# Scaling rows on VectorE ahead of an identity transpose, in place of fp32 matmuls with a diagonal matrix

## The chip, the cores and the metric

One Trainium2 chip, one core. The time is device microseconds (us) of one execution. The engines are TensorE (PE, with its weight loads PEld), VectorE (DVE), ScalarE (ACT), GpSimd (POOL) and SyncE (SP), whose queue issues nearly all transfers. PE's clock has two levels, 1.2 and 2.4 GHz; the profile gives the granted clock as a share of the higher.

## What is computed

One layer of a conditioned decoder trunk on x (256 tokens x 2048 channels, fp32), everything in fp32:

```python
mod = cond @ w_ada[l] + b_ada[l]
sh1, sc1, gt1, sh2, sc2, gt2 = jnp.split(mod, N_MOD, axis=-1)
h = rms_norm(x, g_pre_mix[l]) * (1.0 + sc1) + sh1
y = token_mixing(h, ...)                       # w_in, three branches, gates, w_out
x = x + gt1 * rms_norm(y, g_post_mix[l])       # first residual
h = rms_norm(x, g_pre_ffn[l]) * (1.0 + sc2) + sh2
y = conv_ffn(h, ...)                           # w_up, causal convolution, gelu gate, w_down
x = x + gt2 * rms_norm(y, g_post_ffn[l])
```

rms_norm divides each token's row by the root of its mean square. The two places of the change are the two lines that make h.

## The kernel before

Tokens lie on the partitions for norms and residuals (two halves tt of 128 tokens), channels lie on the partitions for the products. So x (and the residual x2) has to be turned: quarter q of the channels (512) is a tile of 128 x 2 x 512, and its transpose a PSUM tile of four blocks of 128 channels x 256 tokens.

Norm and transpose are one step before. `rstd_from_sums` makes the factor r of each row (reduce and reciprocal on DVE, L195 and L197, root on ACT, L196). `diag_of` (L203) multiplies the identity by r on DVE into d, 128x128 for each half of the tokens. `scaled_transpose` (L210, matmul at L214) multiplies each 128x128 block of x by d, eight matmuls for a quarter; the product is the transposed block with its columns scaled. `make_h2` has the same loop again for quarter 0 (L795), into two PSUM tiles. An fp32 matmul shows as two records on PE, and the trace names these `ptx<-d,x`.

For the input, `x_stats` (L384) makes sums of squares, r1 and d1; `x_transpose(q)` (L391) makes the eight matmuls, ACT copies them out (xn, L394), and `make_h` applies scale and shift and splits into high and low part, hh and hl. For the residual, `residual(tt)` (L771) adds yg*r2 to x (L775, four of 128x512), takes sums of squares on ACT (L201), r3, and d2 for that half. `make_h2(q)` then makes for each of four blocks h2h on ACT (L799), h2f on DVE (L800) and h2l on DVE (L801).

The products are split in three: high x high, low x high, high x low (`mm_b` L231 to L233, `mm_a` L245 to L247). All weights come through SP's queue into four 1 MB buffers (raw), are split by ACT (wh, L274) and DVE (wl, L275; six buffers of each), and used by PE. The conditioning's GEMVs run on PE (gemv, L313) or DVE (L348, L350), and `fin_col` (fin, L286) turns their sums into s and sh columns.

The order of work is a list of items (weight loads with their uses) and calls between them, written out at the end of the kernel; `x_transpose(1..3)` go into a side queue that is served between items, `make_h2` is called twice at the first products of the up-projection and twice later. Parts of the code run at high priority (`out_evac` and `residual` in the last item of the output projection). From this a scheduler fixes each engine's stream when the kernel is built; every engine then runs its stream strictly in order. PSUM tiles of this kind (ps_acc) have three buffers.

Of the kernel before, what the change touches and what calls it, by code (L numbers as in the profile page):

```python
# [46 lines left out]
def kernel(  # L47
# [39 lines left out]

# [1 line left out]
    crow = cp.tile([16, P], F32, name="crow")  # L89
# [51 lines left out]

    # constants that depend on shapes alone
    rcnt = cp.tile([P, 4, 16], F32, name="rcnt")
# [47 lines left out]

# [1 line left out]
    def rstd_from_sums(r, ss, tt):  # L193
# [8 lines left out]

    def diag_of(d, r, tt):  # L203
        nc.vector.tensor_scalar(d[:, tt], ident, r[:, tt:tt + 1], None, op0=ALU.mult)

    def load_sqrt(after):
        """the table of the square root, once `after` is there."""
        nc.scalar.activation(warm, after, AF.Sqrt, bias=eps, scale=0.0)

    def scaled_transpose(xq, d, name):  # L210
        pt = acc_ps(name)
        for a in range(4):
            for tt in range(2):
                nc.tensor.matmul(pt[:, a, tt * 128:tt * 128 + 128],  # L214
                                 xq[:, tt, a * 128:(a + 1) * 128], d[:, tt], start=True, stop=True)
        return pt

# [4 lines left out]
    def mm_b(ps, w, act, first, last):  # L222
        """out channels on partitions: ps[:, nb, :] += w[:, nb*128:].T @ act."""
        n = len(w)
        for i, (wh, wl) in enumerate(w):
            xh, xl = act(i)
            for nb in range(4):
                s = slice(nb * 128, nb * 128 + 128)
                st = first and i == 0 and nb % 2 == 0
                sp = last and i == n - 1  # L230
                nc.tensor.matmul(ps[:, nb], wh[:, s], xh, start=st, stop=False, skip_group_check=True)  # L231
                nc.tensor.matmul(ps[:, nb], wh[:, s], xl, start=False, stop=False, skip_group_check=True)  # L232
                nc.tensor.matmul(ps[:, nb], wl[:, s], xh, start=False, stop=sp, skip_group_check=True)  # L233

    def mm_a(ps, w, act, first, last, tts=(0, 1)):
        """tokens on partitions: ps[:, tt, :] += act[:, tt].T @ w."""
        n = len(w)
        psv = ps.rearrange("p (a b) t -> p a (b t)", a=2)
        for i, (wh, wl) in enumerate(w):
            xh, xl = act(i)  # L240
            for tt in tts:
                s = slice(tt * 128, tt * 128 + 128)
                st = first and i == 0
                sp = last and i == n - 1
                nc.tensor.matmul(psv[:, tt], xh[:, s], wh, start=st, stop=False)  # L245
                nc.tensor.matmul(psv[:, tt], xh[:, s], wl, start=False, stop=False)  # L246
                nc.tensor.matmul(psv[:, tt], xl[:, s], wh, start=False, stop=sp)  # L247

# [1 line left out]
    items = []  # L250
# [30 lines left out]

# [1 line left out]
    def fin_col(src, scale, sec, kt0, n):  # L283
# [14 lines left out]
    def ada_pe(sec, kt0, n):  # L298
        """items: one section's columns kt0*128.., summed over rows on the tensor engine."""
        w = n * P  # L300
# [24 lines left out]
    def ada_dve(sec, kt0, n):  # L325
        """the same, summed over rows on the vector engine."""
        w = n * P
# [48 lines left out]

# [1 line left out]
    ss1 = cp.tile([P, 2, 4], F32, name="ss1")  # L378
    xn = {}

    r1 = cp.tile([P, 2], F32, name="r1")
    d1 = cp.tile([P, 2, P], F32, name="d1", tag="diag")

    def x_stats():  # L384
        for tt in range(2):
            for q in range(4):
                sum_squares(xq[q][:, tt], ss1, q, tt)
            rstd_from_sums(r1, ss1, tt)
            diag_of(d1, r1, tt)

    def x_transpose(q):  # L391
        pt = scaled_transpose(xq[q], d1, "ptx")
        xn[q] = p4(f"xn{q}")
        nc.scalar.activation(xn[q], pt, AF.Copy)  # L394
        del xq[q]
# [19 lines left out]

# [1 line left out]
    part = {}  # L417
# [36 lines left out]
    def block_use(name, kt0, nk, lo, hi):  # L454
        """rows kt0.. of a block's sum over the rows lo to hi."""
        def use(hl_):
# [34 lines left out]
    def block_items(names, lo, hi):  # L491
        """one item for as many neighbouring blocks as make a full load."""
        m = max(1, 4 // (hi - lo))
        while names:
            g = [names[0]]
            while len(g) < min(m, len(names)) and block_cols(names[len(g)]) == block_cols(g[0]) + 512 * len(g):
                g.append(names[len(g)])
            for kt0, nk in pieces(lo, hi):
                w_item(w_in, kt0, nk, block_cols(g[0]), *[block_use(x_, kt0, nk, lo, hi) for x_ in g])
            names = names[len(g):]  # L500
# [7 lines left out]

# [1 line left out]
    yh, yl = {}, {}  # L510
# [197 lines left out]

# [1 line left out]
    mh, ml = {}, {}  # L710
# [19 lines left out]

# [1 line left out]
    ss2 = cp.tile([P, 2, 4], F32, name="ss2")  # L732
# [38 lines left out]
    def residual(tt):  # L771
# [6 lines left out]
        rstd_from_sums(r3, ss3, tt)  # L778
        if tt == 0:
            late["d2"] = cp.tile([P, 2, P], F32, name="d2", tag="diag")  # L780
        diag_of(late["d2"], r3, tt)

    def make_h2(q):
        hh[q], hl[q] = p4(f"h2h{q}", dt=F32R), p4(f"h2l{q}", dt=F32R)
        hf = p4(f"h2f{q}")
        d = late["d2"]
        if q:
            pt = scaled_transpose(x2[q], d, "ptx2")
            pts = [pt[:, o] for o in range(4)]
        else:  # L790
            two = [acc_ps(f"ptx2_{i}") for i in range(2)]
            pts = [two[o // 2][:, (o % 2) * 2] for o in range(4)]
            for o in range(4):
                for tt in range(2):
                    nc.tensor.matmul(pts[o][:, tt * 128:tt * 128 + 128], x2[q][:, tt, o * 128:o * 128 + 128],  # L795
                                     d[:, tt], start=True, stop=True)
        for o in range(4):
# [4 lines left out]

# [1 line left out]
    zc = {}  # L804
# [30 lines left out]
    def up_item(j, half, kt0, lo, hi):  # L835
        """rows kt0.. of a block's sum over the rows lo to hi."""
        key = (j, half)
# [78 lines left out]

# [1 line left out]
    def call(fn):  # L918
        items.append(dict(kind="call", use=fn))

    def mix(a, b, lead=0, skip=0):
        """spread the items of b among those of a, from `skip` to `lead` items before the end."""
        res, bi, n = [], 0, max(1, len(a) - lead - skip)
# [217 lines left out]
```

## Time and profile before

| | us |
|---|---|
| median of three runs | 1440.17 (1439.54 to 1443.15) |
| span of the profiled execution | 1438.6 |
| PE busy | 1399.5 (97%) |
| DVE busy | 1075.6 (75%) |
| ACT busy | 689.0 (48%) |

The profiled execution is given by its span, the time from its first to its last record; the median of the runs is 1.6 us above it. Busy shares are means over stages with different limits, so the sections below go by stretch. In a timeline each row has start, duration, engine, line, operation, result and sources, shape and count, and in brackets how long the engine sat idle before and what ended that. Matmuls are pipelined, so the step from one row to the next is what a row costs, not its duration. ps_up is the up-projection, ps_g the gates' projection, ps_out the output projection.

### The profile page before, as it was taken

What the parts mean: (1) busy time and instruction counts of PE and PEld (TensorE: products, weight loads), DVE (VectorE), ACT (ScalarE), POOL (GpSimd) and SP (SyncE); (2) the same over time, 40 slices, a digit from 0 to 9 for tenths busy, and PEclk for the clock granted to TensorE, in tenths of its full rate; (3) what the DMA queues carried; (4) which work ended last, traced back from release to release, by engine and by line L of the source; (5) the groups of instructions that cost most, each with busy time, mean ns of one, the idle gap of its engine ahead of it and who ended that gap; (6) DMA issues with size and microseconds to landing.
All of it is one profiled execution on the core that took longest, in us unless ns stands there. A gap on an engine that the chain in (4) does not pass through costs nothing.

```text
span 1438.6 us, 24104 instructions
## 1 busy us (share of the span) xinstructions
PE 1399.5 (97%) x10079; PEld 1308.7 (91%) x10079; DVE 1075.6 (75%) x1349; ACT 689.0 (48%) x879; POOL 3.6 (0%) x12
## 2 busy tenths in 40 slices
PE   4999999999999999998999999999999999999997
PEld 3798999999999999887999989898989899999996
DVE  1289878789769977877878876868686766666677
ACT  4552534576744444345346654444444444445453
POOL 0000000000000000000000000000000000000000
PEclk9999999999999999999999999999999999999999
DMA  9799878855877788987976676676676665555551
GB/s 322 288 323 325 295 247 306 276 174 192 303 263 272 271 319 288 345 307 249 364 266 203 207 258 238 207 250 231 220 252 214 238 208 200 178 184 191 183 176 59
DMA packets 183036, 355.76 MB, mean 247 GB/s; under 512 B 5960, under 2 KB 20872, under 8 KB 182928
## 3 DMA queue, kind: packets, MB, share of 16 engines
q1 hardware_dynamic: 182076, 353.07, 72.0%
q8 instruction: 79, 1.29, 0.4%
q10 hardware_dynamic: 852, 1.16, 0.2%
q14 instruction: 29, 0.24, 0.0%
HBM read 352.11 MB, written 2.10 MB: 246 GB/s over the span
## 4 chain that ended last, share of the span: by engine, by line
PE 90%; DMA 4%; DVE 3%; ACT 1%; issue 1%; SPq 0%; DVEq 0%; ACTq 0%
PE ps_up L232 12%; PE ps_up L231 12%; PE ps_up L233 12%; PE ps_g L231 6%; PE ps_g L233 6%; PE ps_g L232 6%; PE ps_dn L246 6%; PE ps_dn L245 6%; PE ps_dn L247 6%; PE ps_out L245 2%; PE ps_out L246 2%; PE ps_out L247 2%; DMA raw<-in_w_in_dram 2%; PE ps_br L231 2%; PE ps_br L232 2%; PE ps_br L233 2%
## 5 line engine op out<-in xcount | busy, mean ns | idle before, releaser
L274 ACT ACTIVATE wh<-raw 128x1024 fp32r<-128x1024 f32 x476 | 489.9, 1037 | 637.7 <-PE ps_up L232 227.1
L275 DVE TENSOR_TENSOR wl<-raw,wh 128x1024 fp32r<-128x1024 f32 x476 | 565.0, 1197 | 243.9 <-ACT wh L274 243.1
L231 PE MATMUL ps_up<-h2h,wh 128*128 128x256 f32 x1408 | 400.2, 284 | 1.2 <-ACT h2h L799 0.8
L232 PE MATMUL ps_up<-h2l,wh 128*128 128x256 f32 x1408 | 399.4, 284 | 0.9 <-DVE h2l L801 0.9
L233 PE MATMUL ps_up<-h2h,wl 128*128 128x256 f32 x1408 | 399.1, 283 | 0.0
L231 PEld LDWEIGHTS ps_up<-h2h,wh 128*128 128x128 f32 x1408 | 270.9, 192 | 2.2 <-ACT h2h L799 0.9
L232 PEld LDWEIGHTS ps_up<-h2l,wh 128*128 128x128 f32 x1408 | 270.8, 192 | 2.1 <-DVE h2l L801 1.4
L233 PEld LDWEIGHTS ps_up<-h2h,wl 128*128 128x128 f32 x1408 | 270.8, 192 | 0.0
L231 PE MATMUL ps_g<-hh,wh 128*128 128x256 f32 x768 | 220.9, 288 | 2.8 <-ACT wh L274 2.8
L233 PE MATMUL ps_g<-hh,wl 128*128 128x256 f32 x768 | 219.0, 285 | 2.6 <-DVE wl L275 2.5
L232 PE MATMUL ps_g<-hl,wh 128*128 128x256 f32 x768 | 218.7, 285 | 0.0
L231 PEld LDWEIGHTS ps_g<-hh,wh 128*128 128x128 f32 x768 | 148.8, 194 | 4.8 <-ACT wh L274 3.8
L233 PEld LDWEIGHTS ps_g<-hh,wl 128*128 128x128 f32 x768 | 148.7, 194 | 3.6 <-DVE wl L275 3.6
L232 PEld LDWEIGHTS ps_g<-hl,wh 128*128 128x128 f32 x768 | 148.7, 194 | 0.3 <-issue 0.2
L245 PE MATMUL ps_dn<-wh,ah 128*128 128x512 f32 x352 | 137.8, 392 | 0.0
L246 PE MATMUL ps_dn<-wl,ah 128*128 128x512 f32 x352 | 137.0, 389 | 0.0
L247 PE MATMUL ps_dn<-wh,al 128*128 128x512 f32 x352 | 136.9, 389 | 0.0
L350 DVE SCALAR_TENSOR_TENSOR accb<-raw,cond,accb 128x512 f32<-128x512 f32 (+1 forms) x147 | 105.8, 720 | 10.4 <-DMA raw<-in_w_ada_dram 10.2
L350 DVE SCALAR_TENSOR_TENSOR acca<-raw,cond,acca 128x512 f32<-128x512 f32 (+1 forms) x155 | 111.9, 722 | 0.1
L245 PEld LDWEIGHTS ps_dn<-wh,ah 128*128 128x128 f32 x352 | 66.1, 188 | 14.0 <-issue 0.5
L246 PEld LDWEIGHTS ps_dn<-wl,ah 128*128 128x128 f32 x352 | 66.1, 188 | 13.9 <-issue 0.5
L247 PEld LDWEIGHTS ps_dn<-wh,al 128*128 128x128 f32 x352 | 66.1, 188 | 13.8
(237 smaller groups left out, 1700.3 us busy)
## 6 DMA issues: line engine op xcount, KB each, us to landing
raw<-in_w_up_dram SPq DMA_DIRECT2D x88, 1024.0 KB
raw<-in_w_ada_dram SPq DMA_DIRECT2D x84, 1024.0 KB
raw<-in_w_in_dram SPq DMA_DIRECT2D x54, 1024.0 KB
raw<-in_w_down_dram SPq DMA_DIRECT2D x44, 1024.0 KB
raw<-in_w_in_dram SPq DMA_DIRECT2D x24, 768.0 KB
raw<-in_w_out_dram SPq DMA_DIRECT2D x16, 1024.0 KB
raw<-in_w_ada_dram SPq DMA_DIRECT2D x16, 768.0 KB
x<-in_x_dram SPq DMA_DIRECT2D x8, 512.0 KB
```

Of the source, the lines that this page charges most:

```text
L231: nc.tensor.matmul(ps[:, nb], wh[:, s], xh, start=st, stop=False, skip_group_check=True)
L232: nc.tensor.matmul(ps[:, nb], wh[:, s], xl, start=False, stop=False, skip_group_check=True)
L233: nc.tensor.matmul(ps[:, nb], wl[:, s], xh, start=False, stop=sp, skip_group_check=True)
L245: nc.tensor.matmul(psv[:, tt], xh[:, s], wh, start=st, stop=False)
L246: nc.tensor.matmul(psv[:, tt], xh[:, s], wl, start=False, stop=False)
L247: nc.tensor.matmul(psv[:, tt], xl[:, s], wh, start=False, stop=sp)
L274: nc.scalar.activation(h[:, :n], it["raw"][:, k:k + n, cs], AF.Copy)
L275: nc.vector.tensor_tensor(l[:, :n], it["raw"][:, k:k + n, cs], h[:, :n].bitcast(F32), op=ALU.subtract)
L350: nc.vector.scalar_tensor_tensor(a, raw[:, kk], sc, a, op0=ALU.mult, op1=ALU.add)
```

## The change

`diag_of` and `scaled_transpose` go, and with them the tiles d1 and d2. `scale_rows` multiplies rows by r on DVE (128x512, one half of the tokens of one quarter), and `transpose_rows` is a PE transpose against the identity. For the input the rows are scaled in place in `x_stats`, all four quarters behind each r. For the residual x2 must stay, so `make_h2(q)` scales into a new tile xs of one quarter, both halves, and transposes that. 64 fp32 matmuls are replaced by 64 transposes. Comments were taken out as well, so line numbers of the changed kernel are 4 or 5 lower after line 208.

```diff
+    def scale_rows(dst, src, r, tt):
+        nc.vector.tensor_scalar(dst[:, tt], src[:, tt], r[:, tt:tt + 1], None, op0=ALU.mult)
-    def diag_of(d, r, tt):
-        nc.vector.tensor_scalar(d[:, tt], ident, r[:, tt:tt + 1], None, op0=ALU.mult)
...
-    def scaled_transpose(xq, d, name):
-        pt = acc_ps(name)
-        for a in range(4):
-            for tt in range(2):
-                nc.tensor.matmul(pt[:, a, tt * 128:tt * 128 + 128],
-                                 xq[:, tt, a * 128:(a + 1) * 128], d[:, tt], start=True, stop=True)
-        return pt
+    def transpose_rows(dst, src, tt, a):
+        nc.tensor.transpose(dst[:, tt * 128:tt * 128 + 128], src[:, tt, a * 128:(a + 1) * 128], ident)
...
     def x_stats():
         for tt in range(2):
             for q in range(4):
                 sum_squares(xq[q][:, tt], ss1, q, tt)
             rstd_from_sums(r1, ss1, tt)
-            diag_of(d1, r1, tt)
+            for q in range(4):
+                scale_rows(xq[q], xq[q], r1, tt)
...
     def x_transpose(q):
-        pt = scaled_transpose(xq[q], d1, "ptx")
+        pt = acc_ps("ptx")
+        for a in range(4):
+            for tt in range(2):
+                transpose_rows(pt[:, a], xq[q], tt, a)
...
         rstd_from_sums(r3, ss3, tt)
-        if tt == 0:
-            late["d2"] = cp.tile([P, 2, P], F32, name="d2", tag="diag")
-        diag_of(late["d2"], r3, tt)
...
         hf = p4(f"h2f{q}")
-        d = late["d2"]
+        xs = p4("xs", (2, 512))
         if q:
-            pt = scaled_transpose(x2[q], d, "ptx2")
+            pt = acc_ps("ptx2")
             pts = [pt[:, o] for o in range(4)]
         else:
             two = [acc_ps(f"ptx2_{i}") for i in range(2)]
             pts = [two[o // 2][:, (o % 2) * 2] for o in range(4)]
-            for o in range(4):
-                for tt in range(2):
-                    nc.tensor.matmul(pts[o][:, tt * 128:tt * 128 + 128], x2[q][:, tt, o * 128:o * 128 + 128],
-                                     d[:, tt], start=True, stop=True)
+        for tt in range(2):
+            scale_rows(xs, x2[q], r3, tt)
+        for o in range(4):
+            for tt in range(2):
+                transpose_rows(pts[o], xs, tt, o)
```

The scheduler's streams differ in a few places. The first is DVE's stream between the second half's evacuation of the output projection and the first blocks of h2 (x is x2, ss and r the sums and factors of both norms; the four x are the quarters). Before:

```order
L275 TENSOR_TENSOR wl<-raw,wh 128x1024
L197 RECIPROCAL r_138<-r_138 128x1
L204 TENSOR_SCALAR d_6681<-ident,r_139 128x128
L775 SCALAR_TENSOR_TENSOR x_6031<-yg_6207,r_138,x_6031 128x512
...
L275 TENSOR_TENSOR wl<-raw,wh 128x1024
L195 TENSOR_REDUCE r_139<-ss_136 128x1
L197 RECIPROCAL r_139<-r_139 128x1
L204 TENSOR_SCALAR d_6681<-ident,r_139 128x128
L800 TENSOR_SCALAR h2f_6731<-ptx_0_6732,s_127,sh_128 128x256
```

And with the change:

```order
L270 TENSOR_TENSOR wl<-raw,wh 128x1024
L204 TENSOR_SCALAR xs<-x_6036,r_138 128x512
L197 RECIPROCAL r_137<-r_137 128x1
L270 TENSOR_TENSOR wl<-raw,wh 128x1024
L773 SCALAR_TENSOR_TENSOR x_6036<-yg_6212,r_137,x_6036 128x512
...
L204 TENSOR_SCALAR xs<-x_6036,r_138 128x512
L796 TENSOR_SCALAR h2f_6733<-ptx_0_6735,s_127,sh_128 128x256
...
L796 TENSOR_SCALAR h2f_6733<-ptx_1_6736,s_127,sh_128 128x256
L204 TENSOR_SCALAR xs<-x_6038,r_138 128x512
L797 TENSOR_TENSOR h2l_6732<-h2f_6733,h2h_6731 128x256
L204 TENSOR_SCALAR xs<-x_6038,r_138 128x512
```

The four residual rows stand behind both weight splits now, and the scaling of quarter 1 (x_6038) stands behind the four h2f of quarter 0. On PE, in the same place, before (ptx_0 and ptx_1 are quarter 0, the other ptx is quarter 1):

```order
L313 MATMUL gemv<-raw,condrep 32x512 x4
L795 MATMUL ptx_0_6732<-d_6681,x_6031 128x128 x3
L795 MATMUL ptx_1_6733<-d_6681,x_6031 128x128 x3
L214 MATMUL ptx_6757<-d_6681,x_6033 128x128 x7
L231 MATMUL ps_up<-h2h_6729,wh 128x256
```

And with the change:

```order
L308 MATMUL gemv<-raw,condrep 32x512 x4
L211 MATMUL ptx_0_6735<-ident,xs 128x128 x3
L211 MATMUL ptx_1_6736<-ident,xs 128x128 x3
L211 MATMUL ptx_6763<-ident,xs 128x128
L226 MATMUL ps_up<-h2h_6731,wh 128x256
L227 MATMUL ps_up<-h2l_6732,wh 128x256
L211 MATMUL ptx_6763<-ident,xs 128x128 x7
L228 MATMUL ps_up<-h2h_6731,wl 128x256
```

The first two ps_up stand inside the transposes of quarter 1, and all others behind them. The third place is PE's stream at quarters 2 and 3. Before, both groups stood inside the ps_up stream of the quarters 0 and 1, about 96 matmuls ahead of fin:

```order
L231 MATMUL ps_up<-h2h_6729,wh 128x256
L214 MATMUL ptx_7637<-d_6681,x_6035 128x128 x8
L232 MATMUL ps_up<-h2l_6730,wh 128x256
...
L214 MATMUL ptx_7661<-d_6681,x_6037 128x128 x8
...
L286 MATMUL fin<-ones,acca 128x1 x4
L231 MATMUL ps_up<-h2h_7634,wh 128x256
```

With the change they stand behind fin:

```order
L281 MATMUL fin<-ones,acca 128x1 x4
L211 MATMUL ptx_7646<-ident,xs 128x128 x8
L211 MATMUL ptx_7673<-ident,xs 128x128
L226 MATMUL ps_up<-h2h_7642,wh 128x256
L227 MATMUL ps_up<-h2l_7643,wh 128x256
L228 MATMUL ps_up<-h2h_7642,wl 128x256
...
L211 MATMUL ptx_7673<-ident,xs 128x128 x7
```

Seven transposes of quarter 3 stand between the fourth and the fifth ps_up of quarter 2. DVE's stream there has, behind fin, two weight splits around the first h2f of quarter 2, and xs of quarter 3 behind its second and third h2f. ACT's has the copy of the transposed input's quarter 1 (xn) ahead of the weight splits of the next blocks, where it stood behind them. The streams of SP and POOL are the same.

## Rows read from the trace of the kernel before

**Rows 1.** The page: busy time by engine, and the chain's shares by engine.

```profile
PE 1399.5 (97%) x10079; PEld 1308.7 (91%) x10079; DVE 1075.6 (75%) x1349; ACT 689.0 (48%) x879; POOL 3.6 (0%) x12
...
PE 90%; DMA 4%; DVE 3%; ACT 1%; issue 1%; SPq 0%; DVEq 0%; ACTq 0%
```

**Rows 2.** Table of stages: stretch, length, busy PE, PEld, DVE, ACT, POOL, clock, DMA share, GB/s.

```profile
100.00:150.00 50.00, 45.06 (x324) 42.88 (x323) 48.64 (x75) 16.82 (x19) 0.00 (x0) 0.94 0.99 330
...
200.00:650.00 450.00, 450.00 (x3359) 427.26 (x3359) 365.15 (x444) 225.25 (x320) 1.09 (x1) 1.00 0.80 274
```

**Rows 3.** The chain, its longest pieces: start, us, what.

```profile
11.93 12.14 DMA raw<-in_w_ada_dram
...
42.26 10.29 DMA raw<-in_w_in_dram
...
80.34 8.79 DMA raw<-in_w_in_dram
```

**Rows 4.** PE's timeline at 730 us: start, us, engine, line, operation, out<-in, count.

```profile
729.82 1.95 PE L214 MATMUL ptx<-d,x 128*128 128x128 f32 x16
731.52 0.36 PE L232 MATMUL ps_up<-h2l,wh 128*128 128x256 f32 x1
```

**Rows 5.** PE's timeline at 310 us.

```profile
309.75 1.03 PE L528 MATMUL pt_w<-ident,sguw 128*128 128x128 f32 x8
310.54 0.36 PE L231 MATMUL ps_g<-hh,wh 128*128 128x256 f32 x1
```

**Rows 6.** DVE's timeline from 658 to 673 us; in brackets idle before and its releaser.

```profile
658.84 1.23 DVE L275 TENSOR_TENSOR wl<-raw,wh 128x1024 fp32r<-128x1024 f32 x1
...
660.06 0.27 DVE L204 TENSOR_SCALAR d<-ident,r 128x128 f32<-128x128 f32 x1
660.25 2.73 DVE L775 SCALAR_TENSOR_TENSOR x<-yg,r,x 128x512 f32<-128x512 f32 x4
...
664.74 0.29 DVE L204 TENSOR_SCALAR d<-ident,r 128x128 f32<-128x128 f32 x1
667.38 0.54 DVE L800 TENSOR_SCALAR h2f<-ptx,s,sh 128x256 f32<-128x256 f32 x1 [2.35 <-ACT h2h L799]
667.96 0.42 DVE L801 TENSOR_TENSOR h2l<-h2f,h2h 128x256 fp32r<-128x256 f32 x1
...
671.96 0.48 DVE L348 TENSOR_SCALAR accb<-raw,cond 128x512 f32<-128x512 f32 x1
672.36 0.41 DVE L801 TENSOR_TENSOR h2l<-h2f,h2h 128x256 fp32r<-128x256 f32 x1
```

**Rows 7.** ACT's timeline at 40 us and at 667 us.

```profile
39.92 1.02 ACT L394 ACTIVATE xn<-ptx 128x1024 f32<-128x1024 f32 x1 [1.16 <-PE ptx L214]
...
666.78 1.74 ACT L799 ACTIVATE h2h<-ptx,sh,s 128x256 fp32r<-128x256 f32 x3 [2.27 <-PE ptx L795]
```

**Rows 8.** PE's timeline from 665 to 670 us.

```profile
665.15 2.26 PE L795 MATMUL ptx<-d,x 128*128 128x128 f32 x12
...
669.34 0.38 PE L231 MATMUL ps_up<-h2h,wh 128*128 128x256 f32 x1 [0.37 <-DVE h2f L800]
...
669.68 0.28 PE L233 MATMUL ps_up<-h2h,wl 128*128 128x256 f32 x1
```

**Rows 9.** PE's timeline from 744 to 752 us.

```profile
744.78 0.95 PE L286 MATMUL fin<-ones,acca 128*128 128x1 f32 x8
746.51 0.38 PE L231 MATMUL ps_up<-h2h,wh 128*128 128x256 f32 x1 [0.78 <-ACT h2h L799]
...
748.01 0.28 PE L232 MATMUL ps_up<-h2l,wh 128*128 128x256 f32 x1
...
748.48 0.41 PE L233 MATMUL ps_up<-h2h,wl 128*128 128x256 f32 x1
...
751.84 0.31 PE L231 MATMUL ps_up<-h2h,wh 128*128 128x256 f32 x1
```

**Rows 10.** Table of stages, the stretch from 750 to 752 us alone.

```profile
750.00:752.00 2.00, 2.00 (x10) 2.00 (x11) 2.00 (x6) 0.74 (x2) 0.00 (x0) 0.53 0.00 0
```

More of the change, by code (lines that the diff above doesn't have):

```diff
@@ L381 @@
     r1 = cp.tile([P, 2], F32, name="r1")
-    d1 = cp.tile([P, 2, P], F32, name="d1", tag="diag")
     def x_stats():
```

## The prediction

> **What bounds the kernel now.** I read the page first, then the stages, then PE's own stream. The page shows PE busy 97% of the span and PE on 90% of the chain that ended last, DMA on 4% [rows 1]. The reader should see that a microsecond of PE work is worth a microsecond only where nothing else ends last. The table of stages says where that is [rows 2]: from 200 to 650 us PE is busy every nanosecond at granted clock 1.00, but from 100 to 150 us it is busy 45.1 of 50 us while DVE works 48.6 and the DMA engines are at 0.99. The chain says the same of the start: three weight transfers of 12.1, 10.3 and 8.8 us lie on it up to 89 us [rows 3]. So PE time that is saved before about 146 us is mostly waited away again, and after it nearly all counts.
>
> The operations that the change touches stand in three places: the start (0 to 65 us: the 32 matmuls on the input), **seam 1** (658 to 670 us: second norm, first two quarters of h2) and **seam 2** (729 to 752 us: quarters 2 and 3). Both seams lie where PE otherwise has no pause, so there I walked PE's and DVE's rows one by one beside the new order.
>
> **What the change saves on PE.** Eight of the old matmuls (16 records, two each) start at 729.82 and the next ps_up follows at 731.52: they push the stream back by 1.70 us, 0.21 each [rows 4]. The nearest row for what takes their place is the transposition of the gating weights, of the same shape and type: 8 transposes, one record each, from 309.75 to the next matmul at 310.54, which is 0.79 us or 0.10 each [rows 5]. So a group of eight gives back 0.91 us, and the eight groups 7.3 us in all. That is the whole gain the change can have, and it is the lower end for the time: 1438.6 - 7.3 = 1431.3.
> The Trainium skill (TensorE: Matmul & The Clock Gate, "Terms") calls the transpose mode four times as fast for FP32; by that, as an estimate, a group would take 0.43 us and the gain be 10.2 us. The rows show 2.2 times (1.70 against 0.79), and I take the rows.
>
> **What it adds on DVE.** Four products ident*r of 128x128 (0.27 to 0.29 us) go; sixteen of 128x512 come (eight on x, eight into xs). Nothing in the trace scales rows by a column at that shape except the first product of the DVE GEMV, 128x512 f32 in SBUF with a scalar per partition: 0.48 us, and the next instruction starts 0.40 us after it [rows 6]. From both sides: 0.29 us (the 128x128 product, the size at a quarter) and 0.75 us (two operands, as in the residual line, 2.73 us for 4, about 0.67 each); I take 0.40 to the next, since kind, shape and memory are those. In sum 16 x 0.40 - 4 x 0.2 = 5.6 us of DVE, whose worth lies only in where they stand.
>
> **The start: 0 us (-2 to +1).** Quarter 0 is ready before the w_ada transfer that lands at 24.07 us [rows 3] both ways; DVE's eight products (3.2 us) have room there. Quarter 1's saving lets PE reach the w_in transfer of 42.26 sooner, but ACT's order changes: the copy of quarter 1's transposes (39.92, 1.02 us, it waited 1.16 us for PE [rows 7]) now stands ahead of the two weight splits for the next blocks, so these and the buffers they free come later. Quarter 2 lies under the 10.29 us transfer, quarter 3's gain (0.91) stands against a similar move of ACT's copies, and the transfers to 144 us would take a rest. I put it at nothing; the cover is the DMA wait. If that cover is gone, three groups count: -2.7, of which I allow -2.
>
> **Seam 1: +4.9 us (3 to 6.5).** Before, DVE goes wl (658.84), d (660.06), residual x4 (660.25), wl, d (664.74) [rows 6]; the second d ends at 665.03 and PE's twelve remaining L795 records start at 665.15 [rows 8]. The quarter-1 matmuls need nothing else, since d serves all quarters: PE runs them straight behind, waits 0.37 for h2f and is in the ps_up stream, whose third matmul starts at 669.68 [rows 8].
> Now the order of DVE is wl, xs(tt0), wl, residual x4, xs(tt1): a product of 0.40 for a d of 0.19, and one weight split (1.15 to the next) that stood behind the residual, beneath ACT's sums of squares, stands ahead of it. The second norm's factor comes 1.35 later, xs another 0.2: PE resumes at about 666.6, +1.45. Its six transposes are half as long as twelve records (2.10 us), so the first h2h starts at about 667.4 (before 666.78 [rows 7]): +0.6.
> The main term comes behind that. Quarter 1's transposes now wait for their own xs, and DVE has that behind four h2f and three h2l of quarter 0 (0.54 and 0.42 us, steps of about 0.48 and 0.37 [rows 6]): 668.0 + 4 x 0.48 + 3 x 0.37 = 671.0 for the first half, and 671.8 to 672.2 for the second behind one more h2l. On PE the engine's order puts one transpose of quarter 1 ahead of the first two ps_up, and seven ahead of the third. So the whole up-projection stands still behind them: third ps_up at 672.2 plus 0.8 to 1.4 = 673.0 to 673.6, against 669.68: **+3.3 to +3.9**.
> The pause costs once more. In seam 2 of before, after pauses of 0.78 and 0.66 us, PE's rows go from 0.28 to 0.41 us from 748.48 to 751.84 [rows 9], at granted clock 0.53, nearly all of it the lower level of 1.2 GHz [rows 10]; rows there are 0.213 apart, not 0.12, so 3.36 us of it lose 1.5 us. Here PE idles from about 667.9 to 671.4, so I take +1.3 of a possible 0.5 to 2.3. Together 3.6 + 1.3 = 4.9.
>
> **Seam 2: +1.4 us (0 to 3).** Before, the 16 old matmuls stood inside the ps_up stream (3.4 us of it, all on the path), so h2 of quarter 2 was waiting only for its shift (fin at 744.78) and the first ps_up came 1.73 us behind fin, the fifth at 748.01 [rows 9]. Now the transposes stand behind fin: 3.4 us less ahead, and h2h waits for ACT's wh, h2f for DVE's wl on both sides (about 1.15 each). With f the start of fin: h2h f+2.2, h2f f+3.4, wl, h2l f+5.0, xs of the last half at f+7.2, seven transposes (0.8 to 1.4), fifth ps_up at f+8.5 to 9.1, where before it was f+3.2. That is 5.3 to 5.9 later; before lost a further 1.7 behind its fifth (0.21 of waiting and 1.5 of clock), now 0.5 to 1.5. Net 4.1 to 5.7 later less 3.4: +0.7 to +2.3, and I take +1.4. If a split on DVE is ready a step earlier it is 0, if the low level lasts as in seam 1 it is 3.
>
> **Elsewhere** the engines' streams are the same, SP's and POOL's queues too; xs takes one buffer of a pool of 25 for a short while. Zero.
>
> **The sum.** 0 + 4.9 + 1.4 = +6.3 on the profiled span: 1438.6 + 6.3 = 1444.9. The median of the runs before (1440.17) is 1.6 us above that span; with that, 1446.5 us. The ends: -2 + 3 + 0 = +1 gives 1441, +1 + 6.5 + 3 = +10.5 gives 1450.7.
>
> **Rivals.** *A, the saved work counts (faster).* PE is the bound, so 7.3 us less the parts beneath transfers (quarters 0 and 2, 1.8 us) come out: 1440.2 - 5.5 = 1434.7. It speaks for this that PE is 97% busy; it decides if every xs is ready before PE reaches its transposes, that is if DVE runs the two quarter-1 products before the h2f of quarter 0. The order of DVE speaks against it: 8 per cent.
> *B, the two cancel (no change).* If the seam's waits come to 3 us or so (DVE's steps shorter, no low clock behind the pause) and the start gives 1 to 2: 1438 to 1443, say 1440.5. For it: half of the terms above are steps of 0.3 to 0.5 us, walked by hand. 20 per cent.
> *C, the low clock lasts (slower still).* Old matmuls kept the seam's PE rows at work until ps_up; now a pause of some 3.5 us ends in a few transposes, and if these don't raise the clock each seam runs another 3.4 us at 0.53, 1.5 us each: 1446.5 + 3 = 1449.5. The trace has transposes only inside a stream at 1.00 [rows 5], so it bears this neither out nor down. 12 per cent.
> The Trainium skill (TensorE: Matmul & The Clock Gate, "Part 4: PE-mode transpose") says that the full clock doesn't engage for transposes; C would be its case, and no row here shows it.
> My forecast has the rest, 60 per cent: a net loss of 3 to 9 us, mostly in seam 1.
>
> **How the numbers follow.** A measurement of this kernel can tell about 0.3% (4.3 us) from no change. Faster than 1435.9: A, 0.08. Within: B, and of the forecast's span the part below +4.3 (0.08), 0.28. Slower: the rest, 0.64. The range goes from 1438 (B's lower half in) to 1451 (the upper end, with C's middle).
>
> **What would show it.** In the profile of the changed kernel: the first ps_up of seam 1 followed by a pause of about a microsecond at its third, released by DVE's xs; PE idle for some 3 us between the quarter-0 transposes and that one, and rows of 0.41 us behind; PE without wait by DVE in the stretch 200 to 650; no ptx inside the ps_up stream at 730; a wait for xs behind fin; PE's records fewer by 64. Wrong would make it: xs ahead of the h2f on DVE; a DVE product of 0.25 us or less; or a start (to 146 us) that ends more than 2 us sooner.

## The result and the profile after

The changed kernel takes 1447.65 us (median of 5 runs, 1445.3 to 1452.37) against 1440.17 us: the medians are 7.5 us apart. The ratio estimated from all runs is 1.0059 (95% interval 1.0043 to 1.0075), so the kernel is 6.2 to 10.8 us slower. The profiled execution has a span of 1444.9 us, 6.3 us over that of before.

First the page of the changed kernel: span, busy time by engine.

```profile
span 1444.9 us, 23994 instructions
...
PE 1395.8 (97%) x10015; PEld 1303.6 (90%) x10015; DVE 1080.8 (75%) x1361; ACT 690.2 (48%) x879; POOL 3.6 (0%) x12
```

PE is busy 3.7 us less than before and DVE 5.2 us more [rows 1]: the work went from PE to DVE as meant, and the time went up. The stages say where; columns as in [rows 2].

```profile
200.00:650.00 450.00, 450.00 (x3359) 427.31 (x3358) 364.25 (x444) 225.59 (x321) 1.09 (x1) 1.00 0.79 274
650.00:700.00 50.00, 41.34 (x284) 34.98 (x280) 41.48 (x72) 25.78 (x47) 0.00 (x0) 0.86 0.75 265
```

From 200 to 650 us PE is busy throughout at clock 1.00, as in [rows 2]. In the 50 us around seam 1 PE is busy only 41.3 us, at a mean granted clock of 0.86; before it was 46.2 us at 0.97. PE's longest waits from 645 to 705 us and from 705 to 780 us (engine, line, what ended the wait: us in total, times, longest) name one cause in both seams:

```profile
PE ptx L211 <- DVE xs L204: 6.5, 3, 3.5
```

```profile
PE ptx L211 <- DVE xs L204: 4.5, 1, 4.5
```

The only other wait of PE in either stretch is for the gemv's transfer, 2.1 us in seam 1, and that was there before (2.0). Seam 1 on PE, answering to [rows 8]:

```profile
660.42 0.44 PE L211 MATMUL ptx<-ident,xs 128*128 128x128 f32 x2 [1.60 <-DVE xs L204]
662.99 1.94 PE L308 MATMUL gemv<-raw,condrep 128*32 128x512 f32 x8 [2.14 <-DMA raw<-in_w_ada_dram]
666.31 1.54 PE L211 MATMUL ptx<-ident,xs 128*128 128x128 f32 x6 [1.38 <-DVE xs L204]
671.39 0.47 PE L211 MATMUL ptx<-ident,xs 128*128 128x128 f32 x1 [3.54 <-DVE xs L204]
671.52 0.56 PE L226 MATMUL ps_up<-h2h,wh 128*128 128x256 f32 x1
...
672.13 1.75 PE L211 MATMUL ptx<-ident,xs 128*128 128x128 f32 x7
673.53 0.56 PE L228 MATMUL ps_up<-h2h,wl 128*128 128x256 f32 x1
...
675.17 0.38 PE L226 MATMUL ps_up<-h2h,wh 128*128 128x256 f32 x1
```

And on DVE, answering to [rows 6] (line numbers are 5, 2 or 4 lower than before, so L270 is the old L275, L773 the old L775, L796 the old L800):

```profile
660.35 1.21 DVE L270 TENSOR_TENSOR wl<-raw,wh 128x1024 fp32r<-128x1024 f32 x1
661.47 2.73 DVE L773 SCALAR_TENSOR_TENSOR x<-yg,r,x 128x512 f32<-128x512 f32 x4
...
665.77 0.49 DVE L204 TENSOR_SCALAR xs<-x,r 128x512 f32<-128x512 f32 x1
...
670.86 0.48 DVE L204 TENSOR_SCALAR xs<-x,r 128x512 f32<-128x512 f32 x1
...
671.58 0.49 DVE L204 TENSOR_SCALAR xs<-x,r 128x512 f32<-128x512 f32 x1
```

One more weight split (660.35) stands ahead of the residual's four rows than before. Quarter 1's two products (670.86, 671.58) stand behind all of quarter 0's h2f, and PE sits idle 3.54 us for the first of them with the whole up-projection behind it. Its third ps_up starts at 673.53, where it was 669.68 [rows 8], and until 675.17 its rows take 0.41 us. The granted clock fell early in the seam, ahead of this pause:

```profile
662.00:664.00 2.00, 1.01 (x8) 0.21 (x8) 2.00 (x4) 1.69 (x5) 0.00 (x0) 0.50 1.05 401
```

It is 0.50 in every stage from 662 to 675 us. Before, it fell in the same place too (0.50 from 664 to 666 us) but was back at 1.00 from 667 on.

Seam 2 on PE, answering to [rows 9], and the granted clock there:

```profile
745.98 0.95 PE L281 MATMUL fin<-ones,acca 128*128 128x1 f32 x8
746.79 1.07 PE L211 MATMUL ptx<-ident,xs 128*128 128x128 f32 x8
752.32 0.45 PE L211 MATMUL ptx<-ident,xs 128*128 128x128 f32 x1 [4.46 <-DVE xs L204]
...
753.42 1.75 PE L211 MATMUL ptx<-ident,xs 128*128 128x128 f32 x7
754.82 0.56 PE L227 MATMUL ps_up<-h2l,wh 128*128 128x256 f32 x1
...
757.32 0.28 PE L226 MATMUL ps_up<-h2h,wh 128*128 128x256 f32 x1
```

```profile
749.00:750.00 1.00, 0.00 (x0) 0.00 (x0) 1.00 (x3) 0.65 (x2) 0.00 (x0) 1.00 0.15 57
...
751.00:752.00 1.00, 0.00 (x0) 0.00 (x0) 1.00 (x3) 0.18 (x1) 0.00 (x0) 0.50 0.01 2
...
756.00:757.00 1.00, 1.00 (x7) 1.00 (x6) 0.79 (x3) 0.56 (x1) 0.00 (x0) 0.50 0.00 0
```

The pause is 4.46 us, again for xs, and the clock falls during it from 1.00 to 0.50, the lower level, and stays there to 757.

Five marks on PE's stream cut the span of every profile into pieces: the last ps_out, the 48th ps_up behind it (by then steps are 0.12 us again), fin of quarter 2, the 48th ps_up behind that, the end. All profiles of the study, in us (the rest is the span, given to a tenth, less the other pieces):

| kernel | to last ps_out | seam 1 | between (ps_up) | seam 2 | rest |
|---|---|---|---|---|---|
| before | 656.69 | 18.39 | 69.70 | 10.19 | 683.63 |
| the change | 656.58 | 23.26 | 66.14 | 15.16 | 683.76 |
| e1 input only | 659.83 | 19.89 | 69.70 | 10.06 | 683.72 |
| e11 the same again | 655.65 | 18.41 | 69.70 | 11.89 | 683.65 |
| e2 residual only | 656.45 | 23.50 | 66.14 | 15.32 | 683.69 |
| e3 scaled early, quarters 0, 1 | 657.71 | 20.65 | 66.14 | 14.33 | 683.77 |
| e4 scaled early, all | 656.29 | 20.50 | 67.88 | 12.67 | 683.76 |
| e5 seam 2 filled, transposes | 657.32 | 23.58 | 66.14 | 12.95 | 683.71 |
| e6 seam 2 filled, matmuls | 660.97 | 24.13 | 66.14 | 12.69 | 683.67 |
| e7 seam 1 filled, transposes | 655.55 | 20.42 | 66.21 | 16.45 | 683.67 |
| e8 seam 1 filled, matmuls | 658.17 | 20.70 | 66.23 | 17.10 | 683.70 |
| e9 as e4, both filled | 658.27 | 18.28 | 67.87 | 10.94 | 683.64 |
| e10 as e9, old input | 654.65 | 18.28 | 67.87 | 10.95 | 683.65 |

The change: seam 1 +4.87, the stream between -3.56 (two groups of old matmuls gone), seam 2 +4.97, the start -0.11, and +0.13 in the rest, which is within the rounding of the spans: +6.3. The first column varies by 5.4 us among kernels with the same input code. All of that arises ahead of 158 us: from the 337th ps_g (at 152 to 158 us) to the last ps_out every profile takes the same time to 0.01 us. A seam of unchanged code varies by up to 1.8 us (before, e1 and e11: 18.39, 19.89 and 18.41 in seam 1, 10.19, 10.06 and 11.89 in seam 2), with how long the clock stays low. So differences of about 1 us in one profile say little; 2 us and more in a seam, with a reason in its rows, do.

### The profile page after: what moved, and what is told of

It reads as the page before. It is cut to its first block, busy times and chain, and to the rows that moved or that the text cites. A ratio compares the mean times of both kernels' runs of the same rounds, so it can differ in the third digit from the quotient of the medians.

```text
span 1444.9 us, 23994 instructions
## 1 busy us (share of the span) xinstructions
PE 1395.8 (97%) x10015; PEld 1303.6 (90%) x10015; DVE 1080.8 (75%) x1361; ACT 690.2 (48%) x879; POOL 3.6 (0%) x12
## 4 chain that ended last, share of the span: by engine, by line
PE 93%; DVE 3%; DMA 2%; ACT 2%; issue 0%; DVEq 0%; SPq 0%; ACTq 0%
PE ps_up L226 12%; PE ps_up L227 12%; PE ps_up L228 12%; PE ps_g L226 6%; PE ps_g L228 6%; PE ps_g L227 6%; PE ps_dn L240 6%; PE ps_dn L241 6%; PE ps_dn L242 6%; PE ps_out L240 2%; PE ps_out L242 2%; PE ps_out L241 2%; PE ps_br L226 2%; PE ps_br L227 2%; PE ps_br L228 2%; DMA raw<-in_w_in_dram 1%
## 5 line engine op out<-in xcount | busy, mean ns | idle before, releaser
L270 DVE TENSOR_TENSOR wl<-raw,wh 128x1024 fp32r<-128x1024 f32 x476 | 564.3, 1196 | 248.3 <-ACT wh L269 247.3
```

Source lines behind the costliest of these rows:

```text
L270: nc.vector.tensor_tensor(l[:, :n], it["raw"][:, k:k + n, cs], h[:, :n].bitcast(F32), op=ALU.subtract)
```

## Experiments

**e1, e2: which half of the change.** Each leaves one half as it was before.

```diff
 e1: residual(), make_h2() as before (diag_of, matmuls with d2)
 e2: x_stats(), x_transpose() as before (diag_of, matmuls with d1)
```

> The input's rows are scaled on DVE and transposed as in the change; the residual keeps the products with d. Theory (the loss comes from the two seams of the residual): within 1.5 us of the kernel before, seams as before (third ps_up of seam 1 about 0.34 us behind the first, fin at 744.8 +-1.5 us). Rival (the start costs: eight products of 0.40 us on DVE and ACT's other order): 3 to 6 us slower, with the shift of PE's rows already there at 200 us.

> The residual part of the change alone; the input keeps d1. Theory: slower than before by about the whole loss, +6.3 us of span (4.9 in seam 1, 1.4 in seam 2), ratio 1.004 to 1.006. Rival (the start costs): no more than 2 us slower.

Measured: input alone 1.0009 (0.9998 to 1.0020), residual alone 1.0057 (1.0040 to 1.0074), beside 1.0059 for both. The residual's half carries the loss, and its two seams in the profile are those of the change (23.50 and 15.32 us). The rival, that the start costs the bulk, is out. Two marks of e1's profile missed: its fin of quarter 2 stood at 749.42 us (744.8 +-1.5 expected), behind a start 3.1 us longer, and its third ps_up 0.54 us behind the first, at the low clock; in e11, the same kernel, they are 743.76 and 0.34.

**e3, e4: the place of the products.** The products for quarters 0 and 1 (e3), or all four (e4), are issued in the residual step behind each r3; `make_h2` then takes these tiles as they are.

```diff
     def residual(tt):
...
         rstd_from_sums(r3, ss3, tt)
+        for q in range(2):              # e4: range(4)
+            if tt == 0:
+                xs_of[q] = p4("xs", (2, 512))
+            scale_rows(xs_of[q], x2[q], r3, tt)
```

> The change, with the products for quarters 0 and 1 of the residual issued in the residual step, right behind each r3, so that quarter 1's stand ahead of quarter 0's h2f on DVE. Theory (place of the products on DVE, not their number): the pause of 3.5 us in seam 1 goes, seam 1 costs +0.5 us (0 to 1.5) against before, seam 2 stays at +1.4: span 1440.5 (1439 to 1442). Rival (the products and transposes cost by themselves, or the clock stays low after transposes): seam 1 stays at +3 or more, span 1443 to 1445.

> The same for all four quarters, in four tiles; the scheduler then puts the transposes of quarters 2 and 3 back inside the ps_up stream. Theory: seam 1 +0.5 to +1.5 us (one weight split and four products between r3's sum and PE), seam 2 -1.8 us (two groups of eight at 0.91 saved in a stream with no pause): span 1437.5 (1436.5 to 1439), in measured time the same as before or up to 0.2% faster. Rival (the clock doesn't hold with transposes in the stream, or DVE's 5.6 us more count): 1441 or more.

Measured: e3 1.0021 (1.0009 to 1.0033), e4 1.0008 (0.9994 to 1.0023). The number of products and transposes is that of the change; the edit moves only their place. e3's seam 1 is 2.61 us shorter than the change's and e4's seam 2 loses its wait for xs, while its stream between saves 1.82 us for two groups, 0.91 each, as estimated. So the place is the main cause. The scheduler moved one more thing, the weight split of 660.35, back behind the residual's rows; that is a small part, since the second half's first xs starts 9.19 us behind the last ps_out in the change, 8.64 in e3 and 8.99 in e4. But both spans missed their expected ranges, by 2.1 and 3.6 us from the middle, and e4's 1441.1 us lies in its rival's range. The rival's first reason doesn't hold: with the transposes of quarters 2 and 3 in the stream the clock is 1.00 from 674 to 748 us. The excess is in the seams. Seam 1 of e4 on PE:

```profile
665.82 3.03 PE L211 MATMUL ptx<-ident,xs 128*128 128x128 f32 x13 [0.73 <-DVE xs L204]
669.38 0.58 PE L226 MATMUL ps_up<-h2h,wh 128*128 128x256 f32 x1 [0.53 <-DVE h2f L803]
...
672.75 0.41 PE L226 MATMUL ps_up<-h2h,wh 128*128 128x256 f32 x1
```

The pause of 3.5 us is gone (0.73 and 0.53 us are left), and the first ps_up starts 13.09 us behind the last ps_out, near the 12.65 of before [rows 8], but the clock is at the lower level and its rows stay at 0.41 us until 673. Of the 2.11 us that the seam takes over before, 0.44 lie ahead of the first ps_up and 1.67 in these rows. Seam 2 of e4, PE, then DVE:

```profile
744.67 0.95 PE L281 MATMUL fin<-ones,acca 128*128 128x1 f32 x8
746.40 0.38 PE L226 MATMUL ps_up<-h2h,wh 128*128 128x256 f32 x1 [0.78 <-ACT h2h L802]
749.07 0.58 PE L227 MATMUL ps_up<-h2l,wh 128*128 128x256 f32 x1 [2.28 <-DVE h2l L804]
...
754.78 0.41 PE L226 MATMUL ps_up<-h2h,wh 128*128 128x256 f32 x1
```

```profile
745.66 0.16 DVE L291 TENSOR_TENSOR sh<-fin,bada 128x4 f32<-128x4 f32 x1 [4.05 <-PE fin L281]
745.74 2.36 DVE L270 TENSOR_TENSOR wl<-raw,wh 128x1024 fp32r<-128x1024 f32 x2
748.02 0.54 DVE L803 TENSOR_SCALAR h2f<-ptx,s,sh 128x256 f32<-128x256 f32 x1
```

Here the scheduler put two weight splits behind the shift (745.66), which waits for fin, and ahead of the first h2f; before, they stood ahead of the shift, where DVE had nothing else to do. The second ps_up waits 2.28 us in place of 0.66, and rows of 0.41 us follow to 755. So the products were not the only thing in the way: an edit here can let the scheduler set a weight split of 1.15 us ahead of what PE waits for, in an order that the kernel's text does not show.

**e5, e6: does the clock fall for the pause, or with transposes?** The pause of seam 2 is filled with work that nobody reads: 40 transposes, or 20 fp32 matmuls as a control.

```diff
         for tt in range(2):
             scale_rows(xs, x2[q], r3, tt)
+        if q == 3:
+            for n in range(40):
+                transpose_rows(pts[n // 2 % 4], last["xs"], n % 2, n // 2 % 4)
+        last["xs"] = xs
```

e5 to e8 ran once each, as profiles (1445.39, 1449.33, 1444.04 and 1448.54 us in whole; e6's start is the longest of all, 660.97 us). They are read by their seams alone.

> The change, with PE's pause in seam 2 (4.5 us, for xs of quarter 3) filled by 40 further transposes of quarter 2's xs, whose results are overwritten. They take about 4 us and nothing waits for them. Theory (the clock falls because PE pauses): the granted clock stays at 1.00 through the filling, ps_up behind it steps by 0.12 us at once, and 1.5 us of the loss go. Rival C (transposes don't hold the clock): the clock falls during or right behind the filling and the rows of 0.41 us stay. The Trainium skill (TensorE: Matmul & The Clock Gate, Part 4: PE-mode transpose) stands on the rival's side.

> The same with 20 fp32 matmuls against the identity (two records each, about 0.21 us) in place of the 40 transposes. Both theories: the clock stays at 1.00 and the rows behind step by 0.12 us. It is the control for the kernel filled with transposes.

Seam 2 filled with transposes, PE and the stages of the granted clock:

```profile
747.85 5.78 PE L211 MATMUL ptx<-ident,xs 128*128 128x128 f32 x49
753.39 0.36 PE L226 MATMUL ps_up<-h2h,wh 128*128 128x256 f32 x1
```

```profile
751.00:752.00 1.00, 1.00 (x11) 1.00 (x10) 1.00 (x2) 0.53 (x1) 0.00 (x0) 1.00 0.54 195
...
753.00:754.00 1.00, 0.99 (x9) 0.75 (x8) 1.00 (x4) 0.45 (x1) 0.00 (x0) 1.00 0.89 129
```

49 transposes in a row, and the clock is 1.00 throughout; the ps_up behind start at 753.39, 753.59, 753.71, 753.83 and go on in steps of 0.12. The control shows the same clock (1.00). Seam 2 takes 12.95 us with transposes and 12.69 with matmuls, against 15.16 and, in e2, 15.32 unfilled. Not all of the 2.2 us need be clock: DVE's xs stand where they stood (fin +5.73 and +6.92), but the scheduler now puts eight ps_up ahead of quarter 3's last seven transposes, not four, and four more at 0.12 us are about 0.5 us in which PE would otherwise wait. So 1.7 to 2.2 us of the seam's loss were clock, lost to the pause (an estimate from these steps).

**e7, e8: do transposes raise the clock once it is low?** The same filling in seam 1, where the clock is already at 0.50: 18 transposes of quarter 0's xs, or 9 matmuls, written with `if q == 1` in the same place.

> The change, with 18 further transposes of quarter 0's xs behind quarter 0's own in seam 1, where the granted clock is already at its lower level (0.50 from 662 us on). With these the scheduler puts 13 ps_up ahead of quarter 1's transposes. Question: do transposes raise the clock? If they count as work: the clock is back at 1.00 by 671 us, about as long after PE's last pause as in the kernel filled with matmuls, and the first ps_up step by 0.12 us. If they don't (rival C): 0.50 through the filling, and rows of 0.41 us for some 3 to 4 us behind it.

> The control: 9 fp32 matmuls against the identity (18 records) in place of the 18 transposes, same place, same order. The clock rises within or right behind the filling under both theories.

PE and the clock of the kernel with transposes, then the clock of the control:

```profile
665.28 4.34 PE L211 MATMUL ptx<-ident,xs 128*128 128x128 f32 x23 [1.11 <-DVE xs L204]
669.38 0.36 PE L226 MATMUL ps_up<-h2h,wh 128*128 128x256 f32 x1
```

```profile
667.00:668.00 1.00, 1.00 (x7) 1.00 (x6) 0.91 (x3) 0.97 (x2) 0.00 (x0) 0.50 1.03 383
668.00:669.00 1.00, 1.00 (x8) 1.00 (x7) 1.00 (x4) 0.96 (x2) 0.00 (x0) 0.68 1.11 401
669.00:670.00 1.00, 1.00 (x11) 1.00 (x10) 1.00 (x4) 0.09 (x1) 0.00 (x0) 1.00 0.98 365
```

```profile
671.00:672.00 1.00, 1.00 (x6) 1.00 (x6) 1.00 (x4) 0.71 (x2) 0.00 (x0) 0.50 1.11 399
672.00:673.00 1.00, 1.00 (x11) 1.00 (x10) 1.00 (x4) 0.00 (x0) 0.00 (x0) 0.96 0.99 367
```

From 665.28 to 669.38 PE does transposes alone, and the clock goes from 0.50 to 1.00 by their end, as it does in the control behind 672. So transposes hold the clock and raise it. Both kernels also put ps_up ahead of quarter 1's transposes; seam 1 falls to 20.42 and 20.70 us, by the clock and by that order together. They give 1.3 and 1.9 us back in seam 2, where the scheduler now sets xs of quarter 2 later and its transposes wait 1.9 us: the same lesson as e4.

**e9, e10: early scaling with the pauses filled.** e9 is e4 with 20 transposes in seam 1 ahead of the last gemv and 24 behind fin; e10 is e9 with the input's half as before.

```diff
+        if q == 0:
+            for n in range(20):
+                transpose_rows(pts[n % 2], xs, 0, n % 2)
...
             nc.scalar.activation(hh[q][:, o], pts[o], AF.Identity, scale=s2[:, k:k + 1], bias=sh2[:, k:k + 1])
+            if q == 2 and o == 0:
+                fill = misc_ps("fill")
+                for n in range(24):
+                    nc.tensor.transpose(fill[:, :128], hh[q][:, 0, :128].bitcast(F32), ident)
```

> All four quarters scaled in the residual step, and PE's pauses at both seams filled with transposes whose results nobody reads (20 in seam 1 ahead of the last gemv, 24 in seam 2 behind fin). Theory (what the early scaling still loses is low clock behind pauses): seam 1 by 1 to 2.5 us and seam 2 by 2 to 2.6 us shorter than with the early scaling alone, span 1437 (1435.5 to 1438.5) at an equal start, measured 0.1 to 0.2% under the kernel before. Rival (the waits for DVE are the loss, not the clock): 1440 or more.

> The residual as in the kernel with early scaling and filled pauses, the input as before (products with d1). Its profile at an equal start was 1.2 us shorter than the kernel before (seam 1 -0.1, the two groups in the stream -1.8, seam 2 +0.7). Theory: span 1437.4 (1436 to 1439), ratio 0.9992 (0.998 to 1.000); if the input's part costs a microsecond or more at the start, it is by that much faster than the filled kernel with the new input. Rival: the start doesn't differ, both have the same ratio.

Measured: e9 1.0001 (0.9991 to 1.0012), e10 0.9991 (0.9979 to 1.0003); spans 1439.0 and 1435.4. PE of e9 at both seams:

```profile
662.17 2.62 PE L211 MATMUL ptx<-ident,xs 128*128 128x128 f32 x22 [1.66 <-DVE xs L204]
...
670.82 0.39 PE L226 MATMUL ps_up<-h2h,wh 128*128 128x256 f32 x1 [1.39 <-DVE h2f L810]
```

```profile
746.15 2.84 PE L809 MATMUL fill<-ident,h2h 128*128 128x128 f32 x24 [0.78 <-ACT h2h L805]
748.75 0.37 PE L226 MATMUL ps_up<-h2h,wh 128*128 128x256 f32 x1
```

Seam 1 is back to 18.28 us and seam 2 to 10.94, 2.2 and 1.7 us shorter than in e4 (1 to 2.5 and 2 to 2.6 were expected). The clock is 1.00 in both seams. With it held, all of the seams' loss but 0.64 us is gone, the two groups in the stream keep their gain, and the kernel's sum behind the start is 1.2 us under that of before. A part of the seams' waits is still there (1.39 us ahead of the first ps_up), so clock and waits together made the loss. The 0.1 to 0.2% that e9 was expected to gain in measured time didn't show, and neither kernel is faster than before by more than its interval; e10, the shortest of all, is at -0.09%, a little short of what this measurement can tell. There is no version here that beats the kernel before beyond doubt.

**e11: the price of the start.** e1 once more, for a narrower interval.

> The input part alone once more, to narrow its price: the first series gave a ratio of 1.0009 (0.9998 to 1.002). Theory as on record (0, from -2 to +1 us): 1.0000 +-0.0010. Rival (the start costs 1 to 2 us): 1.0008 or more.

Measured 1.0013 (1.0000 to 1.0026), after 1.0009; e9 stands 0.0010 over e10, which differs in the input alone. Three comparisons agree on about 0.1%, 1.3 to 1.9 us, and the ten profiles with the new input reach the last ps_out at 657.6 us in the mean, against 655.9 for the three with the old. None of these alone is beyond its noise; together they favour the rival. Where it goes shows at 63 to 75 us. The changed kernel on PE, then ACT:

```profile
63.32 1.05 PE L281 MATMUL fin<-inv,grow 128*128 128x1 f32 x8 [0.72 <-ACT grow L312]
66.70 0.39 PE L226 MATMUL ps_g<-hh,wh 128*128 128x256 f32 x1 [2.32 <-ACT wh L269]
```

```profile
64.61 1.09 ACT L406 ACTIVATE xn<-xn,sh,s 128x256 f32<-128x256 f32 x2 [1.34 <-DVE sh L291]
65.61 1.99 ACT L269 ACTIVATE wh<-raw 128x1024 fp32r<-128x1024 f32 x2
```

fin stands 2.2 us earlier than before (65.52 there), but ACT's two weight splits now follow two scalings that wait for fin, so they start at 65.61 (65.36 before), and PE waits 2.32 us ahead of its first ps_g, where before it waited for nothing. All of the PE time saved on quarters 1 to 3 is waited away there. And the granted clock falls behind that wait. The stage from 60 to 100 us before, then in e11:

```profile
60.00:100.00 40.00, 38.79 (x300) 35.19 (x299) 28.83 (x39) 24.92 (x29) 0.00 (x0) 1.00 0.94 324
```

```profile
60.00:100.00 40.00, 36.81 (x265) 33.91 (x258) 28.57 (x39) 24.30 (x29) 0.00 (x0) 0.91 0.91 309
```

All ten profiles with the new input have the wait (2.32 or 2.33 us), and a granted clock of 0.91 in this stage (0.96 in the change's own). None of the three with the old input has the wait; their clock is 1.00, 1.00 and, in e10, 0.96. From the first ps_g to the 49th it takes 8.1 to 8.9 us with the new input and 6.9, 6.9 and 8.4 with the old, and at the 145th ps_g, near 122 us, the two means are already 1.9 us apart. So the price of the start is there ahead of 122 us, and low clock behind the new wait is likely the main part of it. That isn't shown: no run fills this wait, and e10 shows that the clock can fall here without it.

## Why the prediction held

The forecast of 1446.5 us and the measured 1447.65 differ by 0.1%; the range held it.

- **Seam 1, forecast +4.9: 4.87 us.** Step by step: PE resumed at 666.31 (666.6 forecast), first h2h at 667.25 (667.4), quarter 1's products at 670.86 and 671.58 (671.0 and 671.8), third ps_up at 673.53 (673.0 to 673.6). The clock's part behind the third ps_up was smaller, the rows from there to the thirteenth losing 0.9 us and not 1.3, the wait a little larger. The reason given for it was half right: the clock did not fall in the pause of 3.5 us, it was at 0.50 from 662 us on, after PE's wait of 1.60 us and within that of 2.14, and stayed there through the pause; in e4, without the pause, it stayed low to 673 us all the same. One mark was misplaced: the idle time stood ahead of the first ps_up (the one transpose that precedes it waits for xs), not at the third.
- **Seam 2, forecast +1.4: 4.97 - 3.56 = 1.41 us.** h2h at fin +2.06 (2.2), h2f +3.34 (3.4), h2l +4.93 (5.0), the last xs +6.9 (7.2), fifth ps_up +8.84 (8.5 to 9.1).
- **How much of this is luck.** The marks within 0.3 us are the prediction's own steps. That the two sums agree to some hundredths is luck: e2, with the same seams, has +5.11 and 5.13 - 3.56 = 1.57, and unchanged seams vary by up to 1.8 us.
- **The price of the product**, from the nearest row of the GEMV (0.48 us, 0.40 to the next): xs takes 0.48 and 0.39 to the next. **The saving of a group**, 0.91 us: 1.82 for the two groups of e4.
- **The start, forecast 0 (-2 to +1)**: -0.1 in the profile of the change, but about +1.5 over all runs. This is the term that was mis-sized, by one or two microseconds. The step that was wrong is "a similar move of ACT's copies" for quarter 3, set against the gain with nothing left: the rows show ACT's scalings ahead of the splits, a wait of 2.32 us on PE and low clock behind it, for which the sum had no term at this place. With +1.5 the sum would have been some 1448.
- **The median against the profile.** The medians moved by 7.5 us and the two profiles by 6.3. The start isn't needed to explain that, since e2, with the old input, has the same gap (6.5 us in its profile, 8.2 by its ratio). The profiled execution of the change is one of five, with spans from 1443.6 to 1450.6 us and 1446.6 in the mean, and its granted clock of 0.989 is the highest of them (the others have 0.984 to 0.987).
- **Rival A** (the saved work counts) needed the products ahead of the h2f; with them there (e3, e4) the seams still didn't reach it, for the clock and the weight splits, and with the clock held too (e9) the sum behind the start is only 1.2 us under that of before, not 5.5. **Rival B** fell with the sum. **Rival C** (transposes leave the clock low) is refuted by e5 and e7: the clock held at 1.00 and rose to it in stretches with transposes alone. The low clock is real, 1.7 to 2.2 us of seam 2, but there it comes from the pause.

The Trainium skill (TensorE: Matmul & The Clock Gate, "Part 4: PE-mode transpose") says that the full clock doesn't engage for transposes. These two runs show it engaged (in e5 1.00 from 747 to 753 us; in e7 the rise from 0.50 to 1.00 between 668 and 669 us), so for the fp32 transposes here the measurement decides against the page.

## What to carry to other kernels

Here, moving work from the busiest engine to an idler one could pay only if the new operation had a place in that engine's stream ahead of what the busy engine waits for, and even then the time came out level (e9 1.0001, e10 0.9991); scaling by a diagonal let one small product serve four quarters, and its replacement put a product for each quarter in line behind other work. So read the order of the helping engine at the seams before counting the saved work, and issue such products where their input becomes ready. A pause at a seam was paid twice, once as waiting and once as low clock behind it, and an edit near it can move a neighbour's instructions and lose a good part of what it saves (e7: 2.8 us saved in seam 1, 1.3 lost in seam 2).

## What was not expected

- The granted clock rose from 0.50 to 1.00 during transposes alone (e7), where the prediction had held the opposite possible; and filling a pause with unread transposes gave back 2.2 us (e5: seam 2 12.95 against 15.16 us).
- Early scaling alone (e4) kept seam 1's clock low to 673 us though its pauses ahead of ps_up were only 0.73 and 0.53 us: it had been at 0.50 since the wait for the gemv's transfer, and in the kernel before the seam's work behind that gemv ran without a pause until the clock was back at 1.00 at 667.
- The same instructions in the same order cost 10.06, 10.19 and 11.89 us at seam 2 (e1, before, e11): the fifth ps_up stood at fin +3.23 or +3.24 each time, and only the time behind it differed: the clock was back at 1.00 at fin +6.8, +7.1 and +11.0 us.
